# Ones through TensorE while x is loaded, the first norm's sums later in its stream, a third gate row tile on x without norm, and the last norm's two factors in one step

## The chip, the cores and the metric

The kernel runs on one core of a Trainium2 chip. Its engines are TensorE (PE for matmuls, PEld for the loading of their stationary operand), VectorE (DVE), ScalarE (ACT), GpSimd (POOL) and SyncE (SP), which issues nearly all DMAs. The metric is the device time of one execution in microseconds; runs of the same kernel are told by their median.

## The reference, cut to what matters

One layer of a decoder is run for a prompt of 512 tokens and 8 samples of one token each, 520 columns in all, with 1024 features:

- `xn = rmsnorm(h)`, then `z = xn @ w_in`, 66 row tiles of 128 features and one small tile of 8 gate rows. From z come dilated sliding-window attention (with a cache of keys and values for the samples), an mLSTM of 4 heads behind a causal convolution, the gates `og` of its output, and two more gates.
- `h += (sig(g_a) * P_a(attention) + sig(g_b) * P_b(mLSTM)) @ w_out`
- `h += (silu(xf @ w_gate) * (xf @ w_up)) @ w_down` with `xf = rmsnorm(h)`
- `h += sigmoid(rmsnorm(h) @ w_ple_gate) * (p @ w_ple_proj)`
- `y = rmsnorm(h)`, where rmsnorm is `h / sqrt(mean(h^2) + eps) * g`.

All is kept in f32. A row's factor `1/sqrt(mean + eps)` is the same for all features of a token, so `(x*g) @ w` may be computed first and multiplied by it afterwards.

## The kernel before, in words

Activations lie transposed: features on the 128 partitions, 520 tokens along the free axis, in two halves of 260. Each f32 operand of a dense product is split into a rounded part and a rest (`whi`, `wlo` for weights; `x`, `xnh`, `xnl` and so on for activations), and a product is three matmuls: hi by hi, hi by rest, rest by hi. So a row tile of `w_in` (128 by 1024 weights) is 8 slices by 3 products by 2 halves, 48 matmuls of 260 columns, named `pp<-...` after their PSUM pair. The splits are ACT's (`CAST`) and DVE's (`TENSOR_TENSOR wlo`).

No order is written out by hand. A planner (`Clock`, `on`, `Procs`, `dense_to`, lines 52 to 400) holds its own estimate of each engine's time while the program is built. A list of dense products is walked in order; between matmuls every waiting process (attention, mLSTM, norms, evictions) whose condition holds by that estimate issues its next instructions. All helpers record through line 225, so rows of the profile are told apart by tile names. The order is fixed at build time: on the chip each engine takes its instructions strictly in that order.

At the start x comes in 8 tiles (`xr`). For each, ACT writes `x = xr*g` rounded and DVE the rest (`prep`); ACT also squares each (`sq`) and DVE adds the squares (`first_norm`). `norm` sends the sum of squares through two f32 matmuls with a 128 by 128 tile of ones (`b<-sq,onesr`), which adds over the partitions; ACT takes the root and DVE the reciprocal (`rb`). `renorm` then makes the normalised tiles `xn` (`xnh`, `xnl`). So that TensorE has work before `rb` exists, the gate rows `wg` (36 rows wide) and the first row tiles of `og` (`w_in` rows 42, 43, 44) run on x without norm (`pp<-x,...`), and their evictions multiply by `rb` (`ev_tanh` with False, DVE `th<-pp,rb`, then ACT's tanh). Row tiles on `xn` are evicted by ACT's tanh alone.

After that the list has attention rows, the convolution and value rows of head 0 (`j_head(0)`), more attention rows, head 1, the gate tile `j_mo(1, 1)`, head 2 and so on. The attention of the samples runs in between as a process. Its last part takes the values (`kvb`) of the samples from the cache in four batches: three loads of 256 KB by SP, then four groups of three f32 matmuls of 2 columns each (`b<-pT,kvb`; each is two matmuls in the trace). The tiles come from a ring of 5, so the third load of a batch goes to a tile that the batch ahead still reads.

At the end (`ev_pg`, `last_norm`) each of 8 feature tiles per half gets its last addend. Tiles 0 to 5 are squared by ACT and added up by DVE, and ACT multiplies them by the final gain (`gained`). Tiles 6 and 7 are squared and multiplied by the gain on DVE. The sums go through TensorE, then root, reciprocal, and 8 multiplications by it (`h<-h,rb`), each followed by its store.

Of the kernel before, what the change touches and what calls it, by code (L numbers as in the profile page):

```python
# [10 lines left out]
AF = mybir.ActivationFunctionType  # L11
ALU = mybir.AluOpType
# [217 lines left out]
def _body(nc, a, const, sb, psp, drp):  # L230
    ck = Clock()
    V, S_, G_, PE, SP = (Engine(ck, n, e) for n, e in (
        ("dve", nc.vector), ("act", nc.scalar), ("pool", nc.gpsimd), ("pe", nc.tensor), ("sp", nc.sync)))
# [5 lines left out]
    used = dict.fromkeys(("pp", "G", "WK", "b1", "z", "y", "zc", "yc", "S", "P1", "P2", "cm", "hm", "hf", "sw"), 0)  # L239

    def tl(tag, name, shape=None, dt=F32):
        w = WIDTH.get(tag, 520)
        if tag in used:
            used[tag] += 1
        return ck.new(sb.tile(list(shape or (128, w)), dt, name=name, tag=tag, bufs=NB[tag]), tag, NB[tag])
# [8 lines left out]
    def bank(shape=(128, 512)):  # L254
        used["b1"] += 1
        return ck.new(psp.tile(list(shape), F32, name="b1", tag="b1", bufs=4), "b1", 4)
# [7 lines left out]
    def free(n, tag):  # L264
        used[tag] -= n
# [5 lines left out]
    def on(engs, *tiles, lim=None, **rooms):  # L271

        engs = engs.split()

        def ok():
            for tag, n in rooms.items():
                if tag in used and used[tag] + n > NB[tag]:
                    return False
            now = ck.t["pe"]
            for tag, n in rooms.items():  # L280
                i = ck.count.get(tag, 0)
                if any(ck.idle(tag, i + j, NB[tag]) > now + P["SLACK"] for j in range(n)):
                    return False
            if engs[0] == "pe":
                t = now
            else:
                t = min(ck.t[e] for e in engs)
                if t > now + (P["LIM"] if lim is None else lim):
                    return False
                t = max(t, now) + 0.1  # L290
            return all(ck.ready(x) <= t for x in tiles)
        return ok
# [29 lines left out]
    pr = Procs()  # L322
# [46 lines left out]
    def stt(dst, x, sc, y, op0, op1):  # L369
        V.scalar_tensor_tensor(dst, x, sc, y, op0=op0, op1=op1)  # L370

    def tt(dst, x, y, op):
        V.tensor_tensor(dst, x, y, op=op)

    def mul(dst, x, y):
        tt(dst, x, y, ALU.mult)
# [4 lines left out]
    def square(dst, x):  # L381
        S_.activation(dst, x, AF.Square)
# [33 lines left out]
    def job(chunks, rhs, evac, M=128, group=None, half=None, keep=None, two=False):  # L416

        j = dict(chunks=chunks, rhs=rhs, evac=evac, M=M, keep=keep, two=two, halves=(0, 1) if half is None else (half,), nk=sum(c[2] for c in chunks), i=0)
        jobs.append(j)
        if group is None:  # L420
            order.extend((j, c) for c in range(len(chunks)))
        return j
# [327 lines left out]
    def std(name, m):  # L750
        return [(a[name][m, hf], 4 * hf, 4) for hf in range(2)]
# [4 lines left out]
    gmix, gffn, gple, gfin = (par[:, 8 * i:8 * i + 8] for i in range(4))  # L756
# [6 lines left out]
    onesr = const.tile([128, 128], F32R, name="onesr")  # L763
# [8 lines left out]
    def norm(sq, name):  # L772

        yield on("pe", sq, b1=2)
        bk = [bank() for _ in range(2)]
        for h in range(2):
            PE.matmul(bk[h][:, :TH], ones, sq[:, HS[h]], start=True, stop=True)
        for h in range(2):
            S_.activation(rb[:, HS[h]], bk[h][:, :TH], AF.Sqrt, scale=1.0 / 1024, bias=eps_t)
            V.reciprocal(rb[:, HS[h]], rb[:, HS[h]])  # L780
        free(2, "b1")
        free(1, "y")
        flag[name] = True
# [243 lines left out]
    def ev_tanh(tag, key, scaled=True):  # L1027
        room = {tag: 1} if tag in used else {}

        def gen(ps):  # L1030
            if tag in ("P1", "P2"):
                yield lambda: ("loads", 3) in flag
            if scaled:
                yield on("act", ps, lim=P["EVLIM"], **room)
                t = tl(tag, "th", (128, 520))
                S_.activation(p2(t), ps, AF.Tanh, scale=0.5)
                free(1, "pp")
            else:
                yield lambda: "r0" in flag
                yield on("dve", rb, lim=P["EVLIM"], **room)  # L1040
                t = tl(tag, "th", (128, 520))
                V.tensor_tensor(p2(t), ps, p2(rb), op=ALU.mult)
                free(1, "pp")
                yield on("act", t)
                S_.activation(t, t, AF.Tanh, scale=0.5)
            ml[key] = t
        return gen
# [558 lines left out]
    def j_w(m, evac):  # L1606
        job(std("w_in", m), X, evac)
# [8 lines left out]
    def j_mo(h, vt):  # L1616
        j_w(42 + 2 * h + vt, ev_tanh("OB", ("og", h, vt)))

    group([job([(a["wg"][:, 0:4], 0, 4), (a["wg"][:, 4:8], 4, 4)], X0, ev_gates, M=36, group=1),
           job(std("w_in", 42), X0, ev_tanh("OB", ("og", 0, 0), False), group=1)])  # L1620
    for m in (1, 2):
        job(std("w_in", 42 + m), X0, ev_tanh("OB", ("og", m // 2, m % 2), False))

    n_pre = len(order)
# [1 line left out]
    def j_head(h):  # L1626
        for w in range(2):
            for dt in range(2):
                j_w(18 + 8 * w + 2 * h + dt, ev_conv(h, w, dt))
        for vt in range(2):  # L1630
            j_w(34 + 2 * h + vt, ev_vm(h, vt))
# [4 lines left out]
    for p in range(9):  # L1636
        j_attn(1, p)
    j_head(1)
    j_mo(1, 1)
    j_head(2)  # L1640
    j_mo(2, 0)
    j_head(3)
# [20 lines left out]
    SP.dma_start(nst, a["sn"])  # L1663
    V.memset(eps_t, EPS)
    V.memset(ones, 1.0)
    warm = const.tile([128, 1], F32, name="warm")
    S_.activation(warm, eps_t, AF.Sqrt)

# [165 lines left out]
    def add_sq(x, name, w=520):  # L1834
        yield on("act", x, y=1)
        sq = tl("y", "sq")[:, :w]
        square(sq, x)
        yield on("dve", sq)
        n, acc = ssq.get(name, (0, sq))
        if n:  # L1840
            add(acc, acc, sq)
            free(1, "y")
        ssq[name] = n + 1, acc
# [161 lines left out]
    pe = []  # L2005
# [19 lines left out]

    sq_last = [], []

    def gained(m, hm):
        yield on("act", hm, lim=0.0)
        S_.activation(hm, hm, AF.Copy, scale=gfin[:, m:m + 1])  # L2030

    def ev_pg(m, h):
        def gen(ps):
            ps = ps[0]
            yield lambda: "r3" in flag
            yield on("dve", rb, lim=P["EVLIM"], z=1)
            gs = tl("z", "gs3")[:, :TH]
            V.tensor_tensor(gs, ps, rb[:, HS[h]], op=ALU.mult)
            free(1, "b1")
            yield on("act", gs)  # L2040
            S_.activation(gs, gs, AF.Tanh, scale=0.5)
            if m == 7:
                S_.activation(warm, eps_t, AF.Sqrt)
            yield on("dve", gs, ppt[m])
            stt(gs, gs, 1.0, ppt[m][:, HS[h]], ALU.add, ALU.mult)
            hm = hres[m][:, HS[h]]
            yield on("dve", gs)
            stt(hm, gs, 0.5, hm, ALU.mult, ALU.add)
            free(1, "z")
            if m < 6:  # L2050
                yield from add_sq(hm, ("r4", h), TH)
                pr.spawn(gained(m, hm))
            else:
                yield on("dve", hm, y=1)
                sq = tl("y", "sql")[:, :TH]
                V.tensor_tensor(sq, hm, hm, op=ALU.mult)
                sq_last[h].append(sq)
                yield on("dve", hm)
                V.tensor_scalar(hm, hm, gfin[:, m:m + 1], None, op0=ALU.mult)
        return gen  # L2060

    def last_norm(h):
        yield lambda: ssq.get(("r4", h), (0, 0))[0] == 6
        acc = ssq["r4", h][1]
        yield on("pe", acc, b1=1)
        bk = bank()
        PE.matmul(bk[:, :TH], ones, acc, start=True, stop=False)
        free(1, "y")
        for m in range(2):
            yield lambda: len(sq_last[h]) > m  # L2070
            yield on("pe", sq_last[h][m])
            PE.matmul(bk[:, :TH], ones, sq_last[h][m], start=False, stop=m == 1)
            free(1, "y")
        rl = rb2[:, HS[h]]
        S_.activation(rl, bk[:, :TH], AF.Sqrt, scale=1.0 / 1024, bias=eps_t)
        yield on("dve", rl)
        V.reciprocal(rl, rl)
        free(1, "b1")
        for m in range(8):
            yield on("dve", rl, hres[m])  # L2080
            hm = hres[m][:, HS[h]]
            mul(hm, hm, rl)
            store(a["y"][m][:, HS[h]], hres[m][:, HS[h]], None, S_ if h and m % 2 else SP)

    PEI = lambda: pe
# [45 lines left out]
    for h in range(2):  # L2131
        pr.spawn(last_norm(h))
# [146 lines left out]
```

## Time and profile before

| | us |
|---|---|
| median of 3 runs | 1083.18 |
| lowest, highest | 1081.77, 1091.07 |
| the profiled execution's own time | 1080.5 |
| its span in the trace, first to last instruction | 1078.7 |
| PE busy in the span | 1039.9 (96%) |
| DVE busy | 849.8 (79%) |
| ACT busy | 522.7 (48%) |

Busy times of PE contain the time of matmuls at a lower clock, and neighbouring matmuls overlap, so idle time of PE is read from the waits and not from the difference of two sums. A wait in brackets stands at the instruction that waited, with its length and what ended it. `PEclk` is the granted clock as a share of the full one.

### The profile page before, as it was taken

To read this page: it belongs to the slowest core of one execution; us is meant where nothing else is said; L and a number is where in the kernel's file an instruction comes from. 1 tells how busy PE (TensorE), PEld (TensorE's weight loads), DVE (VectorE), ACT (ScalarE), POOL (GpSimd) and SP (SyncE) were. 2 spreads that over 40 slices of the span, in tenths; PEclk is the share of its full clock that TensorE was granted. 3 is DMA by queue.
4 is the path that set the end of the run, shared out by engine and by line. 5 is a ranking of instruction groups with operands and counts; after the bars stand their busy time and mean duration, and the time that the engine had idled before them with its cause. 6 is when DMAs were issued, how large, how long until landed. Compare 5 with 4: busy or idle time off the path is not lost.

```text
span 1078.7 us, 21787 instructions
## 1 busy us (share of the span) xinstructions
PE 1039.9 (96%) x8416; PEld 1018.9 (94%) x8416; DVE 849.8 (79%) x1757; ACT 522.7 (48%) x970; POOL 36.5 (3%) x126
## 2 busy tenths in 40 slices
PE   7999999999998999999999999999999999999996
PEld 6999899999998998999999999999999999999995
DVE  7995569877778689997566678989888888866785
ACT  6545445554555477765333255444344434433663
POOL 0010110001001011000000000000000000000000
PEclk9999999999998899999999999999999999999999
DMA  6356157765946885966757743422332332333331
GB/s 234 119 187 198 59 165 240 276 192 185 278 154 225 275 310 180 328 220 231 255 172 260 246 125 92 151 82 67 120 95 85 118 102 80 113 89 106 98 112 57
DMA packets 91191, 180.21 MB, mean 167 GB/s; under 512 B 11636, under 2 KB 37796, under 8 KB 89680
## 3 DMA queue, kind: packets, MB, share of 16 engines
q1 hardware_dynamic: 90512, 178.29, 51.0%
q8 instruction: 66, 1.08, 0.4%
q10 hardware_dynamic: 576, 0.53, 0.1%
q14 instruction: 37, 0.30, 0.1%
HBM read 163.65 MB, written 59.13 MB: 207 GB/s over the span
## 4 chain that ended last, share of the span: by engine, by line
PE 70%; DVE 13%; DMA 10%; ACT 3%; issue 3%; SPq 1%; POOL 0%; DVEq 0%; ACTq 0%
PE pp L225 40%; PE b L225 30%; DMA ct<-in_sC 3%; DVE wlo L225 2%; DMA raw<-in_w_in 2%; DVE yc L225 1%; DVE ct L225 1%; DMA kb<-mdr 1%; SPq L225 1%; ACT whi L225 1%; DMA out_kvout<-in_cache 1%; DVE junk L225 1%; DMA out_C_p<-cp 1%; DVE sw L225 1%; DMA qb<-mdr 1%
## 5 line engine op out<-in xcount | busy, mean ns | idle before, releaser
L225 ACT CAST whi<-raw 128x512 fp32r<-128x512 f32 (+3 forms) x346 | 205.6, 598 | 284.1 <-PE pp L225 141.6
L225 DVE TENSOR_TENSOR wlo<-raw,whi 128x512 fp32r<-128x512 f32 (+3 forms) x359 | 236.3, 660 | 134.3 <-ACT whi L225 126.5
L225 PE MATMUL b<-piece,whi 128*128 128x260 f32 x1176 | 212.5, 283 | 1.5 <-DVE whi L225 1.4
L225 PE MATMUL pp<-xnh,whi 128*128 128x260 f32 x1008 | 208.5, 288 | 0.0
L225 PE MATMUL pp<-xnh,wlo 128*128 128x260 f32 x1008 | 207.7, 288 | 0.0
L225 PE MATMUL pp<-xnl,whi 128*128 128x260 f32 x1008 | 204.2, 284 | 0.8 <-DVE xnl L225 0.7
L225 PEld LDWEIGHTS b<-piece,whi 128*128 128x128 f32 x1176 | 181.0, 188 | 1.9 <-issue 1.9
L225 PE MATMUL b<-piece,wlo 128*128 128x260 f32 x588 | 166.1, 283 | 0.1
L225 PEld LDWEIGHTS pp<-xnl,whi 128*128 128x128 f32 x1008 | 157.1, 190 | 1.2 <-DVE xnl L225 1.2
L225 PEld LDWEIGHTS pp<-xnh,wlo 128*128 128x128 f32 x1008 | 157.0, 191 | 1.1
L225 PEld LDWEIGHTS pp<-xnh,whi 128*128 128x128 f32 x1008 | 156.7, 190 | 1.2
L225 PEld LDWEIGHTS b<-piece,wlo 128*128 128x128 f32 x588 | 110.7, 188 | 0.4 <-DVE wlo L225 0.4
L225 PE MATMUL pp<-hpl,whi 128*128 128x260 f32 x352 | 70.8, 283 | 0.0
L225 PE MATMUL pp<-hph,whi 128*128 128x260 f32 x352 | 70.6, 282 | 0.0
L225 PE MATMUL pp<-hph,wlo 128*128 128x260 f32 x352 | 70.6, 282 | 0.0
L225 PEld LDWEIGHTS pp<-hph,wlo 128*128 128x128 f32 x352 | 54.3, 188 | 0.0
L225 PEld LDWEIGHTS pp<-hpl,whi 128*128 128x128 f32 x352 | 54.2, 188 | 0.0
L225 PEld LDWEIGHTS pp<-hph,whi 128*128 128x128 f32 x352 | 54.2, 188 | 0.0
L225 ACT CAST whi<-ws 128x512 fp32r<-128x512 f32 x28 | 17.4, 622 | 57.5 <-PE b L225 48.5
L225 DVE SCALAR_TENSOR_TENSOR yc<-zc,par,yc 128x552 f32<-128x552 f32 x48 | 37.7, 786 | 5.1 <-ACT yc L225 4.5
L225 DVE TENSOR_TENSOR uv<-uv,b 128x260 f32<-128x260 f32 (+1 forms) x84 | 40.7, 485 | 0.0
L225 PE MATMUL b<-x3h,wlo 128*128 128x260 f32 x128 | 36.5, 285 | 0.0
(389 smaller groups left out, 1906.3 us busy)
## 6 DMA issues: line engine op xcount, KB each, us to landing
raw<-in_w_in SPq DMA_DIRECT2D x132, 256.0 KB, 2.7
out_kvout<-in_cache SPq DMA_DIRECT2D x64, 512.0 KB, 5.0
raw<-in_w_gate SPq DMA_DIRECT2D x44, 256.0 KB, 4.0
raw<-in_w_up SPq DMA_DIRECT2D x44, 256.0 KB, 3.9
ct<-in_sC SPq DMA_DIRECT2D x32, 256.0 KB, 6.4
out_C_s<-ct SPq DMA_DIRECT2D x32, 256.0 KB, 5.4
raw<-in_w_down SPq DMA_DIRECT2D x32, 256.0 KB, 2.7
out_kvout<-in_cache SPq DMA_DIRECT2D x16, 510.0 KB, 4.8
```

The source lines that it names most:

```text
L225: fn(*args, **kw)
```

## The change

Four edits:

- After the tile of ones is set, 24 matmuls of ones by ones (128 columns) are issued into a PSUM bank that nobody reads.
- `norm` for the first norm waits, in the planner's estimate, until TensorE's time is 1.5 us past the time at which the sum of squares is ready.
- Row tile 45 (`og`, head 1, second half) runs on x without norm with the first three, and is taken out of its place between head 1 and head 2.
- `gained` and its two counterparts on DVE go; the 8 multiplications by the reciprocal become `scalar_tensor_tensor` steps that multiply by the gain (one value per partition, from `par`) and by the reciprocal. The square of tile 6 goes from DVE to ACT.

```diff
@@ norm
         yield on("pe", sq, b1=2)
+        if name == "r0":
+            yield lambda: ck.ready(sq) + 1.5 <= ck.t["pe"] and used["b1"] <= 2
         bk = [bank() for _ in range(2)]
@@ the list of dense products
-    for m in (1, 2):
+    for m in (1, 2, 3):
         job(std("w_in", 42 + m), X0, ev_tanh("OB", ("og", m // 2, m % 2), False))
...
     j_head(1)
-    j_mo(1, 1)
     j_head(2)
@@ start
     V.memset(ones, 1.0)
+
+    wb = bank((128, 128))
+    for _ in range(24):
+        PE.matmul(wb, onesr, onesr, start=True, stop=True)
+    free(1, "b1")
@@ end
-    def gained(m, hm):
-        yield on("act", hm, lim=0.0)
-        S_.activation(hm, hm, AF.Copy, scale=gfin[:, m:m + 1])
...
             if m < 6:
                 yield from add_sq(hm, ("r4", h), TH)
-                pr.spawn(gained(m, hm))
             else:
-                yield on("dve", hm, y=1)
+                yield on("act" if m == 6 else "dve", hm, y=1)
                 sq = tl("y", "sql")[:, :TH]
-                V.tensor_tensor(sq, hm, hm, op=ALU.mult)
+                if m == 6:
+                    square(sq, hm)
+                else:
+                    V.tensor_tensor(sq, hm, hm, op=ALU.mult)
                 sq_last[h].append(sq)
-                yield on("dve", hm)
-                V.tensor_scalar(hm, hm, gfin[:, m:m + 1], None, op0=ALU.mult)
...
-            mul(hm, hm, rl)
+            stt(hm, hm, gfin[:, m:m + 1], rl, ALU.mult, ALU.mult)
```

Since the planner's estimate shifts, the order moves in more places than the edits. Three are shown.

TensorE at the start, before: the norm's two matmuls (`b_294`, `b_295`) stand right behind the gate rows (the 36-wide matmuls), ahead of the second half of the first `og` tile.

```order
L225 MATMUL pp<-x_196,whi 36x260 x2
L225 MATMUL pp<-x_197,whi 36x260 x2
L225 MATMUL pp<-x_196,wlo 36x260 x2
L225 MATMUL b_294<-sq,onesr 128x260
L225 MATMUL b_295<-sq,onesr 128x260
L225 MATMUL pp<-x_174,whi 128x260 x2
L225 MATMUL pp<-x_175,whi 128x260 x2
L225 MATMUL pp<-x_174,wlo 128x260 x2
```

And in the change (`b_330`, `b_331`):

```order
L225 MATMUL pp<-x_221,wlo 36x260 x2
L225 MATMUL pp<-x_199,whi 128x260 x2
L225 MATMUL pp<-x_200,whi 128x260 x2
L225 MATMUL pp<-x_199,wlo 128x260 x2
L225 MATMUL pp<-x_207,whi 128x260 x2
L225 MATMUL pp<-x_208,whi 128x260 x2
L225 MATMUL b_330<-sq,onesr 128x260
L225 MATMUL b_331<-sq,onesr 128x260
L225 MATMUL pp<-x_207,wlo 128x260 x2
```

Ten matmuls of the `og` tile have moved ahead of the norm's two.

TensorE at the fourth and last batch of the samples' values, before: 40 dense matmuls (20 rows, of which the last two stand here) lie between the third batch and the fourth, and the fourth's groups of three have dense matmuls between them.

```order
L225 MATMUL pp<-xnh,whi 128x260 x2
L225 MATMUL pp<-xnl,whi 128x260 x2
L225 MATMUL b_4403<-pT,kvb 128x2 x3
L225 MATMUL pp<-xnh,wlo 128x260 x2
L225 MATMUL b_4403<-pT,kvb 128x2 x3
L225 MATMUL pp<-xnh,whi 128x260 x2
L225 MATMUL pp<-xnl,whi 128x260 x2
L225 MATMUL b_4403<-pT,kvb 128x2 x3
L225 MATMUL pp<-xnh,wlo 128x260 x2
L225 MATMUL b_4403<-pT,kvb 128x2 x3
```

In the change the third batch (`b_4423`) and the fourth (`b_4491`):

```order
L225 MATMUL b_4356<-pT,kvb 128x2 x3
L225 MATMUL pp<-xnh,whi 128x260 x2
L225 MATMUL pp<-xnl,whi 128x260 x2
L225 MATMUL pp<-xnh,wlo 128x260 x2
L225 MATMUL pp<-xnh,whi 128x260 x2
L225 MATMUL pp<-xnl,whi 128x260 x2
L225 MATMUL pp<-xnh,wlo 128x260 x2
L225 MATMUL b_4423<-pT,kvb 128x2 x12
L225 MATMUL pp<-xnh,whi 128x260 x2
L225 MATMUL pp<-xnl,whi 128x260 x2
L225 MATMUL pp<-xnh,wlo 128x260 x2
L225 MATMUL pp<-xnh,whi 128x260 x2
```

Between the second batch (its last group is `b_4356`) and the third there are now 12 dense matmuls, and between the third and the fourth 10 of them and four transposes (`b<-cstA,yc`). From the first batch's first group to the fourth's last there were 124 dense matmuls, and there are 50.

DVE at the end, before: behind the last matmul of the last tile (`gs_14097<-b_14060`), the square and the gain of tile 6 (`h_7928`) and of tile 7 (`h_7930`), then the reciprocal and the multiplications.

```order
L225 TENSOR_TENSOR gs_14097<-b_14060,rb 128x260
L225 TENSOR_TENSOR sq<-sq 128x260
L225 TENSOR_TENSOR sql<-h_7928 128x260
L225 TENSOR_SCALAR h_7928<-h_7928,par 128x260
L225 SCALAR_TENSOR_TENSOR gs_14097<-gs_14097,ppt 128x260
L225 SCALAR_TENSOR_TENSOR h_7930<-gs_14097,h_7930 128x260
L225 TENSOR_TENSOR sql<-h_7930 128x260
L225 TENSOR_SCALAR h_7930<-h_7930,par 128x260
L225 RECIPROCAL rb_13286<-rb_13286 128x260
L225 TENSOR_TENSOR h_7916<-h_7916,rb_13286 128x260
```

And in the change:

```order
L225 TENSOR_TENSOR gs_14110<-b_14074,rb 128x260
L225 TENSOR_TENSOR sq<-sq 128x260
L225 SCALAR_TENSOR_TENSOR gs_14110<-gs_14110,ppt 128x260
L225 SCALAR_TENSOR_TENSOR h_7956<-gs_14110,h_7956 128x260
L225 TENSOR_TENSOR sql<-h_7956 128x260
L225 RECIPROCAL rb_13312<-rb_13312 128x260
L225 SCALAR_TENSOR_TENSOR h_7942<-h_7942,par,rb_13312 128x260
```

Three instructions have left this piece, and each of the 8 multiplications reads a second factor from `par`.

## Rows read from the trace of the kernel before

**Rows 1.** The page's first part: busy time, share, instructions of each engine.

```profile
PE 1039.9 (96%) x8416; PEld 1018.9 (94%) x8416; DVE 849.8 (79%) x1757; ACT 522.7 (48%) x970; POOL 36.5 (3%) x126
```

**Rows 2.** Stretches: busy us (count) of PE, PEld, DVE, ACT, POOL; clock; DMA.

```profile
270.00:485.00 215.00, 204.18 (x1585) 197.97 (x1584) 179.70 (x451) 130.30 (x235) 15.52 (x59) 0.97 0.75 247
485.00:1040.00 555.00, 552.12 (x4582) 549.88 (x4581) 435.71 (x775) 237.73 (x423) 0.00 (x0) 1.00 0.42 135
```

**Rows 3.** Timeline, 0 to 20 us: start, us, engine, out<-in, count, idle before.

```profile
0.84 0.17 DVE L225 MEMSET onesr<- 128x128 f32 x1
5.23 1.44 PE L225 MATMUL pp<-x,whi 128*36 128x260 f32 x4 [5.23 <-ACT x L225]
...
8.83 1.07 PE L225 MATMUL pp<-x,whi 128*36 128x260 f32 x4
...
12.48 0.64 PE L225 MATMUL pp<-x,whi 128*128 128x260 f32 x4
...
14.18 4.71 DVE L225 TENSOR_TENSOR sq<-sq 128x520 f32<-128x520 f32 x6
...
17.27 0.40 PE L225 MATMUL pp<-x,wlo 128*36 128x260 f32 x2
...
18.95 1.14 PE L225 MATMUL b<-sq,onesr 128*128 128x260 f32 x4 [1.28 <-DVE sq L225]
```

**Rows 4.** Timeline, 34 to 41 us, TensorE on the first normalised tiles.

```profile
34.26 0.40 PE L225 MATMUL pp<-xnh,whi 128*128 128x260 f32 x2
...
38.92 0.51 PE L225 MATMUL pp<-xnl,whi 128*128 128x260 f32 x2 [0.65 <-DVE xnl L225]
...
40.74 0.51 PE L225 MATMUL pp<-xnl,whi 128*128 128x260 f32 x2
```

**Rows 5.** Timeline and tile view of the samples' values (kvb), 316 to 338 us.

```profile
316.71 0.72 PE L225 MATMUL b<-pT,kvb 128*128 128x2 f32 x6
...
317.01 0.37 SPq L225 DMA_DIRECT2D kvb<-in_cache  x1
...
320.72 0.72 PE L225 MATMUL b<-pT,kvb 128*128 128x2 f32 x6
...
337.08 0.38 PE L225 MATMUL b<-pT,kvb 128*128 128x2 f32 x2 [0.67 <-DMA kvb<-in_cache]
...
DMA to landing us min/median/max: 4.8/4.9/5.0
```

**Rows 6.** Two stretches of 5 us right behind it.

```profile
340.00:345.00 5.00, 5.00 (x24) 5.00 (x25) 2.29 (x5) 2.66 (x4) 0.66 (x2) 0.50 1.04 401
350.00:355.00 5.00, 3.72 (x18) 3.75 (x19) 4.90 (x16) 1.67 (x3) 0.00 (x0) 0.51 0.61 180
```

**Rows 7.** Waits of TensorE, 345 to 370 us: us in total, times, longest.

```profile
PE b L225 <- DVE nout L225: 1.5, 1, 1.5
PE b L225 <- POOL qkm L225: 1.5, 1, 1.5
```

**Rows 8.** Timeline, 1066 us to the end.

```profile
1067.28 0.42 ACT L225 ACTIVATE gs<-gs 128x260 f32<-128x260 f32 x1 [0.55 <-DVE gs L225]
1067.50 0.42 DVE L225 TENSOR_TENSOR sql<-h 128x260 f32<-128x260 f32 x1
...
1068.23 0.42 DVE L225 SCALAR_TENSOR_TENSOR gs<-gs,ppt 128x260 f32<-128x260 f32 x1
...
1070.89 1.78 DVE L225 RECIPROCAL rb<-rb 128x260 f32<-128x260 f32 x1 [0.92 <-ACT rb L225]
1072.70 2.81 DVE L225 TENSOR_TENSOR h<-h,rb 128x260 f32<-128x260 f32 x8
```

**Rows 9.** Groups by form on DVE: busy us, mean ns, idle before.

```profile
L225 DVE SCALAR_TENSOR_TENSOR xn<-xr,par,rb 128x520 f32<-128x520 f32 x8 | 5.8, 751 | 0.0
...
L225 DVE SCALAR_TENSOR_TENSOR th<-th,pp 128x520 f32<-128x520 f32 x8 | 5.5, 688 | 0.0
L225 DVE TENSOR_TENSOR xnl<-xn,xnh 128x520 fp32r<-128x520 f32 x8 | 5.2, 693 | 0.6 <-ACT xnh L225 0.6
```

## The prediction

> **What bounds the kernel now.** I read first the page's busy times: PE is busy for 1039.9 of 1078.7 us, the next engine, DVE, for 849.8 [rows 1]. A change can win only where TensorE stands still or runs at a lower clock. The stretches say where: from 485 to 1040 us 4582 matmuls fill 555 us, 0.121 us for each, with next to no gap, while from 270 to 485 us PE is busy for 204 of 215 us and the granted clock is 0.97 on the mean [rows 2]. The timeline gives the places that this change touches: the start, the hand-over to the normalised tiles, the attention of the samples around 316 to 338 us, and the tail.
>
> **Start.** The first gate matmul waits until 5.23 us for x. From 8.83 four matmuls take 1.07 us, from 12.48 only 0.64 [rows 3]: a step of 0.217 us against 0.12. The step of 0.217 is that of the lower level (1.2 GHz); it ends between these rows. At 17.27 the last two gate matmuls start, and the norm's sums then wait for DVE until 18.95, for 1.28 us [rows 3].
>
> *24 matmuls of ones.* They can start once the tile of ones is set, at 1.01 us. At 0.121 us each they take 2.9 us, at 0.217 us 5.2 us, so they end between 3.9 and 6.2 us. The late end would push the first gate matmul by 1.0 us. That is covered: between 5.23 and 8.83 us 12 matmuls with 2.6 us of steps take 3.6 us, which leaves 1.0 us idle. A full clock before 8.83 would bring TensorE to the norm's sums sooner, but the sums wait for the sixth addition of squares on DVE (14.18 to 18.89 us) [rows 3], which is fed by x and by ACT and takes nothing from TensorE. So the term is 0 whether or not the clock rises. Without that cover it would be 1.0 us of loss at most, or, if DVE ended earlier, up to 1.0 us of gain.
>
> *Norm's sums later.* Ten matmuls now stand ahead of them: 10 x 0.121 = 1.2 us. Even at the old pace TensorE is through them at 17.51 + 1.21 = 18.72, before 18.95. The sums start when they did, ACT's root and DVE's reciprocal come when they did, and ten matmuls are done: **-1.2 us**. If the sums were ready earlier, their delay would pass to the reciprocal instead.
>
> *Third row tile on x.* Its 48 matmuls are moved, not added. The first normalised matmul, at 34.26 before, comes 48 x 0.121 - 1.2 = 4.6 us later. In front of the last rest `xnl` DVE has one eviction and one weight rest more, 0.69 us each. So the rests come 1.4 us later and their user 4.6 us later, and the wait of 0.65 at 38.92 goes. From 34.26 to 40.74 us 44 matmuls took 6.48 us where 44 x 0.121 = 5.32 would do [rows 4]: **-1.2 us**. The tile's two loads of 256 KB, ACT's two casts and a cache copy move with it; the third row tile's weights are due only 48 matmuls later than the second's, so I cost them at nothing. If they were late, the bound is the 0.65 of the old wait.
>
> **Where the tile is taken out.** This part is dear, and it is no edit: the order shows it. The tile was 5.8 us of work that needs nothing from DVE but its weights, between two heads. Without it the planner puts the samples' four batches into 50 dense matmuls instead of 124. The third load of a batch is issued only once the batch ahead has read its tile: at 317.01, in the last group of the second batch (316.71). A load lands after 4.9 us where its landing was waited for; the group at 320.72, though, waited for nothing, so its third matmul at about 321.2 had its tile after 4.2 us [rows 5]. With 4.9, the third tile is there 5.2 us after the last group's start. In the new order TensorE can fill of this, for batch 2 to 3: the group 0.73, 12 x 0.121 = 1.45, two pairs of the next group 0.48, in all 2.66, wait 2.5 us. Batch 3 to 4: 0.73, 10 x 0.121, four transposes at a dense matmul's step 0.48, and 0.48, in all 2.9, wait 2.3. (Batch 1 to 2 has a dozen mLSTM matmuls between; I take it as covered.) Together 4.8 us against 1.0 before, of which the longer was 0.67 [rows 5]: **+3.8**; with 4.2 us for a landing 3.4, +2.4. I take the middle, +3.1. Against it: while TensorE stands, DVE and POOL go on, and the waits right behind, 1.5 for `nout` and 1.5 for `qkm` [rows 7], can shrink by 0 to 3.0 us; I take half, -1.5. The granted clock was 0.50 from 340 to 345 and 0.51 from 350 to 355 us [rows 6], after TensorE had done the 2-column matmuls with few dense ones between; over the stretch to 485 us 3% of 215, 6.5 us, were lost so [rows 2]. I expect this again, and take 0 for the difference (from -6.5 to +6.5). Sum here **+1.6 us**.
>
> **Tail.** Behind the last tanh (1067.28 + 0.42 = 1067.70) DVE is still at tile 6's square and gain, and goes on at 1068.23 [rows 8]. Both leave: the chain is 0.5 us earlier. Tile 6's square on ACT takes the place of one of ACT's gain steps, ahead of the tanh; hidden. Then 8 steps follow the reciprocal on the path. One that reads a factor per partition takes 751 ns on 128x520, one with a constant 688, a plain product 693 [rows 9]: 0.06 us for the factor, 8 x 0.06 = 0.5 us. Sum **0** (-0.5 if the factor costs nothing on 260 columns). ACT's dozen gain steps in the first half ran beside a TensorE without waits, so they give nothing.
>
> Here a rule speaks against the change. The rows have a `scalar_tensor_tensor` with a constant as fast as a product (688 and 693 ns), both from two f32 sources [rows 9]. The Trainium skill, "Vector Engine (DVE) Microarchitecture Reference", section "Points that are easy to get wrong", says that this instruction with two SBUF sources that are not bf16 runs at half the rate. The trace's `xn<-xr,par,rb` has two such sources and 751 ns, so it does not agree.
>
> **The sum.** The profiled execution took 1080.5 us (span 1078.7), 2.7 below the median of 1083.18. -1.2 - 1.2 + 1.6 + 0 = -0.8: 1079.7 for it, and against the median **1082.4 us**: no change. This kernel's runs differ by some 0.9% (1081.77 to 1091.07), so what is within 1% can't be told from no change.
>
> **Rivals.**
> 1. *Slower: the samples' values hold TensorE, and its clock.* The waits of 4.8 us stand, none behind shrinks, and the emptier stretch keeps the lower level for as long again: -2.4 + 3.8 + 6.5 = +7.9, **1091.1**. For it: only 22 dense matmuls lie between the last three batches. Against: at half clock the matmuls in between fill more of each landing. It decides as soon as waits and lost clock grow by over 2.4 us together. Chance 0.17.
> 2. *Faster: the clock holds.* The two low stretches followed a certain mixture, which is gone; without them -6.5: -2.4 + 1.6 - 6.5 = -7.3, **1075.9**. For it: both were short. Against: the new mixture has fewer columns. Chance 0.10.
> 3. *The start gives nothing.* The planner's 1.5 us is its own estimate; if DVE's additions end early on the chip, the reciprocal is late by what the ten matmuls take, and the old waits come back: +1.6 alone, **1084.8**. Against: 18.95 is set by x. Chance 0.13.
> 4. *The final steps take double.* As a mechanism of this kernel: 8 steps of 0.35 (2.81 for 8 [rows 8]) become 0.70, +2.8 in place of +0.5: -0.8 + 2.3 = +1.5, **1084.7**. Rows 9 speak against it. Chance 0.03. This is what the skill's sentence above would make of it.
>
> The forecast keeps 0.57; its own bounds, from 4.2 us landings with all waits behind gone and the tail's half us (-3.5) to the full waits (+1.4), give 1080 to 1085. The range takes in rival 2 and most of rival 1: **1076 to 1090**. Faster by over 1% (under 1072.3) needs rival 2 with the low bounds, 0.05; slower by over 1% (over 1094) rival 1 with the tail or start lost too, 0.07; within 1%, 0.88.
>
> **What the new profile would show.** Sums still at about 18.95 with a shorter or no wait, ten `x` matmuls ahead; a step of 0.12 before 8.83 us if the ones raise the clock; no wait on `xnl` near 43 us; waits on `kvb` of 3 to 5 us in all, near 320 to 345 us; on ACT no `h<-h,par`; final steps of about 0.41 us on a chain 0.5 us earlier. I am wrong if TensorE waits for `kvb` no longer than before, if the sums start later than 19.5, or if the low clock covers less than 5 or more than 25 us.

## The result: 1% faster, and the profile after

The changed kernel takes 1073.0 us (median of 11 executions, 1070.81 to 1079.78) beside 1083.37 us (median of 11, 1080.26 to 1091.07) on the same chip: a ratio of 0.990, with a 95% interval of 0.9876 to 0.9924. I had forecast 1082.4 us and a range of 1076 to 1090. The gain of 10.4 us is over ten times the 0.8 us of my sum, and most of what the traces place of it lies where my sum had no term.

The profiled executions took 1080.5 us (span 1078.7) and 1072.9 us (span 1071.1). The spans show 7.6 us. The other 2.8 us are that the profiled execution of before lies below its median and the one of after at its own.

The page's first part, after, answers to [rows 1]. The 24 matmuls more are the ones; TensorE's busy time is 1.1 us longer, the span 7.6 us shorter, so it is waiting that went.

```profile
PE 1041.0 (97%) x8440; PEld 1022.7 (95%) x8440; DVE 848.3 (79%) x1749; ACT 518.3 (48%) x963; POOL 40.8 (4%) x126
```

The stretches of after (columns as in [rows 2]): from 485 us on nothing has changed, and the clock from 270 to 485 is no better than before, 0.96 beside 0.97.

```profile
270.00:485.00 215.00, 205.56 (x1604) 200.20 (x1603) 184.08 (x458) 131.57 (x237) 20.41 (x59) 0.96 0.77 249
485.00:1040.00 555.00, 552.45 (x4577) 550.10 (x4577) 435.86 (x778) 237.86 (x420) 0.00 (x0) 1.00 0.41 132
```

**Where the 7.6 us lie.** Since matmuls stand in another order, I compare the start of the same matmul in both timelines and take off 0.121 us for each dense matmul (`pp<-...`) that the change has done more by then (the count is that of the order). What is left is called net below. Four marks do: the first scores of head 0 (`kh,qh`), the end of its attention (`t,cstB`), head 2's `vmh,kwh` and the last `nt`. In the timeline of before:

```profile
91.95 0.33 PE L225 MATMUL b<-kh,qh 64*128 64x128 f32 x1
...
131.40 1.03 PE L225 MATMUL b<-t,cstB 128*128 128x8 f32 x8 [1.45 <-ACT whi L225]
...
367.46 0.28 PE L225 MATMUL b<-vmh,kwh 128*128 128x256 f32 x1
...
478.59 0.62 PE L225 MATMUL b<-nt,onesr 128*128 128x16 f32 x4 [0.55 <-DVE nt L225]
```

And of after:

```profile
97.69 0.33 PE L225 MATMUL b<-kh,qh 64*128 64x128 f32 x1
...
132.67 1.06 PE L225 MATMUL b<-t,cstB 128*128 128x8 f32 x8 [0.25 <-DVE t L225]
...
362.78 0.28 PE L225 MATMUL b<-vmh,kwh 128*128 128x256 f32 x1
...
482.95 0.62 PE L225 MATMUL b<-nt,onesr 128*128 128x16 f32 x4
```

| up to (us, before) | shift | dense matmuls more | net | in this stretch |
|---|---|---|---|---|
| 91.95 | +5.74 | 54 | -0.8 | -0.8 (start) |
| 131.40 | +1.27 | 52 | -5.0 | **-4.2** (head 0's attention) |
| 367.46 | -4.68 | -6 | -4.0 | +1.1 (with the place of the tile taken out) |
| 478.59 | +4.36 | 96 | -7.3 | **-3.3** (heads 2 and 3) |
| 1078.7, end | -7.6 | 0 | -7.6 | -0.3 (with the tail) |

Each column rests on one execution, so I looked at how far executions with one order differ. The kernels with the ones alone and with the end alone (below) have before's order on TensorE up to 1041 us. In their profiled executions head 0's attention takes as long as in that of before within 0.05 us, and the stretch from 367 to 479 us within 0.4 us; but from 131 to 367 us they take 1.8 and 3.4 us longer. So the +1.1 can't be told from nothing, and the 2.8 us that the spans don't show may lie in that stretch; no run shows that they do. A second execution with the change's order (without the ones, below) has -4.2 and -2.7 in the two bold rows.

**Head 0's attention.** Before, 12 transposes of `P` stand in one batch on TensorE:

```
405 L225 MATMUL b_1516<-cstA,P 128x128 x4
406 L225 MATMUL b_1526<-cstA,P 128x128 x4
407 L225 MATMUL b_1536<-cstA,P 128x128 x4
408 L225 MATMUL pp<-xnh,wlo 128x260 x2
```

They take 2.66 us there (116.11 to 118.77), 0.22 each, where four of them at 106.39 took 0.36, 0.09 each. The timelines of TensorE and ACT show why: ACT makes one exponential of `P` in 0.49 us, and each pair of transposes waits for the next one.

```profile
106.39 0.60 PE L225 MATMUL b<-cstA,P 128*128 128x128 f32 x4
106.75 0.49 PE L225 MATMUL pp<-xnh,wlo 128*128 128x260 f32 x2
...
116.11 2.90 PE L225 MATMUL b<-cstA,P 128*128 128x128 f32 x12
118.77 0.48 PE L225 MATMUL pp<-xnh,wlo 128*128 128x260 f32 x2
```

```profile
115.97 0.49 ACT L225 ACTIVATE P<-P,st 128x256 f32<-128x256 f32 x1
...
116.46 0.49 ACT L225 ACTIVATE P<-P,st 128x256 f32<-128x256 f32 x1
...
116.95 0.49 ACT L225 ACTIVATE P<-P,st 128x256 f32<-128x256 f32 x1
```

The list of the matmuls' waits doesn't show them: the modelled end of a matmul, 0.33 us behind its start, covers all but 0.05 us of each gap, while the weight load of the next pair shows 0.3 us. Waits of before from 92 to 138 us (total, times, longest), of the matmuls and of the weight loads:

```profile
PE b L225 <- ACT whi L225: 1.5, 1, 1.5
PE b L225 <- DVE st L225: 0.8, 1, 0.8
PE b L225 <- DVE E L225: 0.4, 1, 0.4
...
PEld b L225 <- ACT P L225: 1.5, 5, 0.3
```

After, no more than two such groups of four stand in a row, and between the others lie other products. All that is left of the waits in the same stretch:

```profile
PE b L225 <- DVE t L225: 0.3, 1, 0.3
PE b L225 <- DVE E L225: 0.2, 1, 0.2
```

That is 2.7 + 1.5 us of waits before and 0.5 after: 3.7 of the 4.2 us. The 1.5 us put down to `whi` stand at the matmul `t,cstB`, which reads `t`. DVE had finished `t` only 0.1 us ahead of that matmul, so DVE's steps up to `t` alone would have held it nearly as long:

```profile
131.11 0.19 DVE L225 TENSOR_TENSOR t<-ex,cstB 128x32 f32<-128x32 f32 x1
```

### The profile page after: what moved, and what is told of

It reads as the page before. It is cut to its first block, busy times and chain, and to the rows that moved or that the text cites. A ratio compares the mean times of both kernels' runs of the same rounds, so it can differ in the third digit from the quotient of the medians.

```text
span 1071.1 us, 21842 instructions
## 1 busy us (share of the span) xinstructions
PE 1041.0 (97%) x8440; PEld 1022.7 (95%) x8440; DVE 848.3 (79%) x1749; ACT 518.3 (48%) x963; POOL 40.8 (4%) x126
## 4 chain that ended last, share of the span: by engine, by line
PE 77%; DVE 12%; DMA 5%; ACT 3%; issue 2%; SPq 0%; POOL 0%; DVEq 0%; ACTq 0%
PE pp L225 45%; PE b L225 32%; DMA raw<-in_w_in 2%; DVE wlo L225 2%; DMA ct<-in_sC 2%; DVE yc L225 2%; DVE ct L225 1%; DVE sw L225 1%; DVE Wf L225 1%; ACT whi L225 1%; DVE z L225 1%; DVE junk L225 1%; SPq L225 0%; DMA kvb<-in_cache 0%; DMA xr<-in_xT 0%
## 5 line engine op out<-in xcount | busy, mean ns | idle before, releaser
L225 PE MATMUL pp<-xnh,whi 128*128 128x260 f32 x992 | 204.2, 287 | 0.0
L225 PE MATMUL pp<-xnh,wlo 128*128 128x260 f32 x992 | 203.5, 287 | 0.0
L225 PE MATMUL pp<-xnl,whi 128*128 128x260 f32 x992 | 199.7, 283 | 0.0
L225 PEld LDWEIGHTS pp<-xnh,wlo 128*128 128x128 f32 x992 | 153.7, 190 | 1.0
L225 PEld LDWEIGHTS pp<-xnh,whi 128*128 128x128 f32 x992 | 153.0, 189 | 1.3
L225 PEld LDWEIGHTS pp<-xnl,whi 128*128 128x128 f32 x992 | 153.5, 189 | 0.0
```

Source lines behind the costliest of these rows:

```text
L225: fn(*args, **kw)
```

## The experiments

Theory A: the order in which the planner puts the attention between the dense matmuls sets the time, and the edits act mostly by shifting the planner's own clock. Theory B: the edits act on the chip (the clock raised by the ones, the fuller start). One thing has to be added to the words on the planner: its estimate sets more than the order. For copies, casts and some multiplications `pick` takes ACT or DVE, whichever the planner thinks is done first. Of the 359 casts `whi<-raw`, DVE has 13 in the trace of before, 15 in that of the change, and 13 to 23 in those below. So "the order" means the order and this choice. Ratios are to the kernel before, with 95% intervals, from up to 12 executions each.

**Each edit alone.** Four kernels, each with one of the four edits of the diff shown above and nothing else.

> The 24 matmuls of ones alone; the order of all other matmuls stays as before. Theory A (the gain of 7.6 us in the profiled spans comes from what the moved tile does to the order of work in head 0's attention, 92 to 131 us, and in the stretch from 287 to 480 us): TensorE reaches the step of 0.12 before 10 us instead of 11.4 to 12, but the norm's sums still wait for DVE's additions and start at 18.9 to 19.4; the time is that of before within 1 us (ratio 0.999 to 1.001). Theory B (the ones raise the clock early and this is carried through to the end): at least 2 us less (ratio 0.998 or lower).

Measured: 0.9997 (0.9982 to 1.0013). TensorE's order is that of before up to 1041 us; the step of 0.12 is there from 11.0 us (before from 12.2), not before 10, and the sums start at 19.22, behind a wait for DVE of 1.9 us (before 1.3). What the ones are worth on the chip can't be told from zero.

> Only the norm's sums are put later, behind ten matmuls of the second row tile on x; the order up to head 0's attention is otherwise as before, but from about 290 us on the planner places a few matmuls otherwise. Theory A: the ten matmuls wait for their own weights, which ACT casts and DVE rests only behind the squares and additions, so the sums start 1 to 2 us later than 18.95 and nothing is won: 0 to +1.5 us (ratio 0.999 to 1.002). My prediction's step: sums at 18.95, 1.2 us less. Theory C (any shift of the planner's clock rolls the order of the attention anew): a difference of 2 us or more of either sign, in the stretch behind 290 us.

Measured: 0.9973 (0.9947 to 0.9999). The sums start at 20.38, 1.4 us later than before, as theory A says, and by 91.95 us the kernel is 0.7 us behind; yet the time is 0.1 to 5.7 us less. What brings that, if it is more than the spread of executions, must lie behind 290 us: at 287 us the kernel is level with before. The one profile (1085.3 us, above this kernel's median of 1083.8) doesn't show it: open.

> Only the row tile is moved (done on x, at the start, and taken out between head 1 and head 2). The order in head 0's attention changes, though not into that of the whole change. Theory A: this alone brings most of the gain, 5 to 8 us less (ratio 0.992 to 0.9955): no waits on xnl near 40 us, and in head 0's attention the transposes of P no longer wait one by one for ACT (2.66 us for 12 before). Theory B: less than 2 us. My prediction's steps for it: -1.2 at the start and +1.6 behind, +0.4.

Measured: 0.9964 (0.9941 to 0.9988), between the theories' numbers. By 131.40 us the tile alone has won 5.0 us net, as much as the whole change. By 256 us (head 1's first `st,E`) it has lost them all again: in head 1's attention TensorE waits 1.7 us for `t`, 0.9 for `pt`, 0.7 for `E`, 0.6 for `P`.

> Only the end is changed (the last norm's two factors in one step, tile 6's square on ACT); the order up to the last matmuls is as before. The chain of the tail is 0.5 us shorter up to the reciprocal. If a factor per partition costs 0.06 us a step, the 8 final steps take 0.5 us more and the sum is 0; if it costs nothing on 260 columns, -0.4 to -0.5; if the step runs at half rate, 8 steps of 0.7 us, +2.3. All theories: within 1 us of before but for the last (ratio 1.002).

Measured: 0.9999 (0.9978 to 1.0021). Nothing that can be told from zero.

The four alone sum to -0.67%; together they give -1.0%. The intervals of the four are too wide to tell these two numbers apart. The next four take parts out.

**The change without the ones** (the loop over `PE.matmul(wb, onesr, onesr, ...)` and its bank are left out).

> The whole change without the 24 matmuls of ones. TensorE's order in head 0's attention is that of the change, behind 290 us a little different. Theory A (the gain is in the order of the attention, not at the start): still 8 to 11 us less than before (ratio 0.990 to 0.9925), with no more than 1 us of waits in 80 to 135 us. Theory B (the ones, by the clock, carry a part that only shows together with the other edits): 5 us less than before or fewer (ratio 0.995 or higher).

Measured: **1.0105** (1.0086 to 1.0125), 1095.8 us. Both theories missed. Up to 290 us it is ahead of the change (net -7.0 at 286.79, where the change has -4.2), then it loses 22 us. In the program it differs from the change by the ones and by the order: on DVE from 252 us, on TensorE from 273 us. Either could be the cause; the pair further down tells them apart.

**The change with the sums where they were** (the two lines in `norm` are left out).

> The whole change with the norm's sums where they were. TensorE's order in head 0's and head 1's attention is now that of the kernel with the moved tile alone, which lost in head 1's attention what it won in head 0's. Theory A (orders decide): 4 to 5 us less than before (ratio 0.995 to 0.9965), with 4 us or more of waits in 190 to 270 us. Theory D (the later sums are a gain by their own work at the start): the first normalised matmul comes 1.2 us later than in the change and nothing else differs, 9 us less than before (ratio 0.9915).

Measured: 0.9959 (0.9931 to 0.9987). As theory A says: TensorE's order in head 0 and head 1 is that of the kernel with the tile alone, and so are the loss in head 1 and the time.

**The taking-out alone.**

```diff
-    j_mo(1, 1)
     j_head(2)
+    j_mo(1, 1)
     j_mo(2, 0)
```

> The kernel before with the row tile taken out between head 1 and head 2, as in the change, but done behind head 2 and not at the start: the order up to 315 us is as before. It measures the taking-out alone, for which my prediction had +1.6 us (waits on kvb 3 to 5 us in all). Theory A' (taking it out costs nothing or gains, since the attention of the samples and head 2 then hide otherwise): 0 to -3 us (ratio 0.997 to 1.000). My prediction's step: ratio 1.0015 with waits on kvb of 3 us or more.

Measured: 1.0006 (0.9986 to 1.0026). The interval holds 0 and my +1.6 us; but the waits on `kvb` are 0.6 us, not 3 to 5. In their place stands a wait of 4.0 us on `nout`. TensorE's waits of this kernel from 270 to 485 us:

```profile
PE b L225 <- DVE nout L225: 6.2, 4, 4.0
...
PE b L225 <- DMA kvb<-in_cache: 0.6, 1, 0.6
```

**The tile ahead of head 0, but on the normalised x.**

```diff
+    j_mo(1, 1)
     for p in range(9):
         j_attn(0, p)
...
     j_head(1)
-    j_mo(1, 1)
```

> The kernel before with the row tile as the first on the normalised x, in place of the third on x without the norm: its 48 matmuls stand ahead of head 0 as in the change, but not at the start. The order in head 0's attention changes once more. Theory A (any order with the waits in head 0's attention spread wins): the waits in 80 to 135 us (2.9 before, and 1.5 more of weight loads that wait for ACT's exponentials) fall by 2 us or more and the time by 2 to 5 us. Theory E (it is the three tiles without the norm, with DVE free of the normalised rests, that win): the wait on xnl at 38.9 us stays and the time is that of before within 1 us (ratio 0.999 to 1.001).

Measured: **1.0142** (1.0111 to 1.0173). Neither theory's number. The wait on `xnl` stays, as said. But "any order wins" is false: here the batch stays (the weight loads wait 1.5 us for `P`), and head 1's attention loses more.

**The order apart from the instructions.** The planner's estimate can be moved without adding or removing work on the chip. In the first kernel it is told of the ones, but they aren't issued; in the second they are issued and it isn't told:

```diff
-        PE.matmul(wb, onesr, onesr, start=True, stop=True)
+        ck.emit("pe", "matmul", (wb, onesr, onesr), {})
```

```diff
-        PE.matmul(wb, onesr, onesr, start=True, stop=True)
+        nc.tensor.matmul(wb, onesr, onesr, start=True, stop=True)
```

> The whole change, with the planner told of the 24 matmuls of ones but none of them issued: TensorE's order is that of the change, row for row, without the ones. It differs from the change without ones (10.5 us slower than before) in the order behind 290 us alone. Theory A (the order that the planner ends with sets the time, not the ones on the chip): like the change, 8 to 12 us less than before (ratio 0.989 to 0.9925). Theory B (the ones on the chip matter): 5 us or more above the change, towards the 1095 us of the change without ones.

> The counterpart: the 24 matmuls of ones are issued, but the planner isn't told of them, so that the order is that of the change without ones. Theory A: 1094 to 1097 us, ratio 1.009 to 1.012, with the same waits behind 310 us (z 5 us, th 4 us) and the same low clock. Theory B: like the change, 1073.

Measured: 0.9900 (0.9866 to 0.9935), 1074.2 us, and 1.0117 (1.0079 to 1.0155), 1097.4 us. Theory A, on both sides. The order of the change without the ones is as fast as the change; the ones without their order are as slow as the change without ones. So of the kernels without ones the one takes 1074.2 and the other 1095.8 us with the same work, ten copies, casts and multiplications of which stand on the other one of ACT and DVE. By the ratios (0.9900 and 1.0105) that is **some 22 us from the order behind 250 us alone**. How much of it the choice of engine brings, no run tells apart. Two stretches of each (columns as in [rows 2]), first the slow one, then the fast one:

```profile
290.00:370.00 80.00, 73.20 (x489) 70.77 (x488) 56.22 (x129) 33.67 (x59) 7.87 (x26) 0.79 0.62 189
...
485.00:620.00 135.00, 125.38 (x975) 123.34 (x974) 87.77 (x176) 54.21 (x95) 0.00 (x0) 0.94 0.65 220
```

```profile
290.00:370.00 80.00, 73.77 (x555) 71.67 (x554) 61.08 (x144) 36.39 (x64) 7.72 (x26) 0.89 0.67 218
...
485.00:620.00 135.00, 133.35 (x1096) 132.67 (x1095) 87.80 (x163) 53.49 (x97) 0.00 (x0) 0.99 0.68 232
```

TensorE is busy as long from 290 to 370 us in both, but at a granted clock of 0.79 against 0.89: 66 matmuls fewer. The slow one's waits from 290 to 620 us name what it stood for:

```profile
PE b L225 <- ACT z L225: 6.3, 3, 5.3
PE pp L225 <- ACT th L225: 4.5, 1, 4.5
PE b L225 <- DVE piece L225: 2.6, 2, 1.8
```

The same means gives two more orders. The kernel **before**, with the planner told of 36 ones that aren't issued:

> The kernel before with the planner told of 36 matmuls of ones that aren't issued, and nothing else: the same instructions as before in another order, which in head 0's attention is that of the kernel with the moved tile alone. Theory A: the waits in head 0's attention fall as they did there, 3 to 4 us won by 131 us; what the new order does further on isn't known (that kernel lost it again in head 1's attention), and the time differs from before by up to 5 us either way, with no change in the work. Theory F (it is the tile done on x ahead of head 0 that takes the waits away, not the order): the stretch up to 131 us takes as long as before within 1 us.

Measured: **1.0090** (1.0059 to 1.0121). No work is added or removed on the chip (14 copies, casts and multiplications go from ACT to DVE and 10 from DVE to ACT), and the time is 10.9 us longer. At the start it loses 3.0 us net: the first gate matmul, at 5.23 us before, comes at 9.40. In this order ACT has the cast of the first `w_in` weights ahead of the first x, and it waits 3.5 us for their load; before, ACT writes the first x at 4.45. ACT in this kernel:

```profile
8.10 0.62 ACT L225 CAST whi<-raw 128x512 fp32r<-128x512 f32 x1 [3.52 <-DMA raw<-in_w_in]
8.62 2.58 ACT L225 ACTIVATE x<-xr,par 128x520 fp32r<-128x520 f32 x4
```

In head 0 the order wins 3.4 us, as said. In head 1 a batch of the same kind forms, with waits of 0.7 us for `pt` and 1.2 for `P`, and then the clock falls: from 235 to 270 us it is 0.71, where before has 1.00. Its profiled rows:

```profile
235.00:270.00 35.00, 31.23 (x172) 28.42 (x172) 19.92 (x54) 12.25 (x35) 2.09 (x6) 0.71 0.46 141
```

The **change**, told of 36 in place of 24 and without the ones on the chip, which puts the batch of 12 back into head 0:

> The change with the planner told of 36 matmuls of ones in place of 24 (none issued): from head 1 on the order is that of the change, but in head 0's attention the 12 transposes of P stand in one batch again, as in the kernel before. Theory A (the batch is what TensorE waited in): 2.5 us for the 12 transposes again and waits of 2 us or more in 80 to 135 us, 3 to 5 us more than the change (ratio to before 0.993 to 0.995). Rival (the gain up to 131 us is the moved work and not the batch): like the change, 0.9900 +- 0.0015.

Measured: 0.9981 (0.9957 to 1.0006): 7.7 us of the gain are gone, more than the 3 to 5 of the theory. The weight loads wait 1.5 us for `P` again, in 5 pieces, and the matmuls 0.8 for `st`, 0.9 for `zc`, 0.4 for `E`. That is the batch's own part, 3.7 us by the table below. The rest has a place too. Against the change with no ones issued, the profiled execution loses 2.0 us net ahead of head 0 (ACT has the cast of the first weights ahead of the first x here too, and the first gate matmul comes at 10.12 us, in that one at 5.35) and 2.2 from 131 to 226 us. These and the batch make 7.8 us. Behind 226 us every engine has the order of the change; the 6.6 us that this execution still loses there (5.7 of them from 287 to 367 us, at a granted clock of 0.82 against 0.89) come from something else, and they are about what it lies above this kernel's median (1088.9 against 1081.9).

**Head 0 in all kernels.** The stretch from the first `kh,qh` to the first `t,cstB`, by TensorE's order in it, with 0.121 us for each dense matmul above or below 126:

| TensorE's order in head 0 | kernels | us | dense | at 126 |
|---|---|---|---|---|
| that of before | before, ones, sums later, end, tile later | 39.45 to 39.49 | 126 | 39.5 |
| change, batch put back | 1 | 37.19 | 112 | 38.9 |
| tile first on the normalised x | 1 | 37.55 | 100 | 40.7 |
| that of the tile alone | tile moved, no sums later, before in another order | 40.13 to 40.14 | 160 | 36.0 |
| that of the change | the change and three without ones or with the planner not told | 34.97 to 34.98 | 124 | 35.2 |

Within a row of several kernels ACT, DVE and POOL have one order in this stretch too. Kernels with different edits and one order agree within 0.04 us; kernels with nearly the same edits and another order differ by 3 to 5. For this stretch that settles it. For 367 to 479 us, where the change wins 3.3 us, no kernel changes that part alone, and it stays argued: the waits there on `nt`, `qkm`, `W3l`, `sqhh` and `sqhl` (3.2 us before from 370 to 485) are nearly gone (0.3), one on `nout` is 0.9 us longer, and one of 0.4 on `W2l` is new.

## Why the prediction was wrong, step by step

- **The step that failed is one that I didn't take.** The sum had terms for the start, for the place where the tile is taken out, and for the tail. Head 0's attention had none: I took the tile as 5.8 us that come earlier and push the rest along, although the order shows the batch of `P` dissolved. The waits there stood in the profile of before, 1.5 put down to `whi`, 0.8 on `st`, and 1.5 more among the weight loads. It is worth -4.2 us here. The new order in heads 2 and 3, -3.3 us, had no term either.
- *Matmuls of ones, 0.* Right on the chip, for the reason given: DVE's additions cover them. They ran from 1.07 to 6.25 us, at the late end of my bounds, and the second tile of x came 0.5 us later in this execution. The step falls from 0.217 to some 0.13 at 9.35 us, and before only at 12.24. I called the step of 0.217 the lower level, and the rows don't bear that out: the granted clock reads 1.00 from 0 to 16 us in both traces, whatever the step. Wrong as a part of the change: in the planner they decide some 22 us.
- *Norm's sums later, -1.2.* Wrong; I had named 19.5 us as the limit, and they start at 20.72. I counted the ten matmuls' columns and not their weights. ACT casts these behind the squares and DVE makes the rests behind the additions, and so both wait in front of the sums. TensorE at the start, after:

```profile
1.07 5.38 PE L225 MATMUL b<-onesr 128*128 128x128 f32 x24 [1.07 <-DVE onesr L225]
...
18.06 0.74 PE L225 MATMUL pp<-x,whi 128*128 128x260 f32 x4 [0.80 <-ACT whi L225]
19.90 0.51 PE L225 MATMUL pp<-x,wlo 128*128 128x260 f32 x2 [1.10 <-DVE wlo L225]
...
20.72 1.04 PE L225 MATMUL b<-sq,onesr 128*128 128x260 f32 x4
```

- *Third row tile on x, -1.2.* Right: no wait on `xnl` is left (from 40.47 to 46 us the pairs of matmuls follow one another every 0.24 us). With the sums' delay the first normalised matmul comes at 40.47, 6.2 us later in place of 4.6; so the start gives -0.8 and not -2.4. This is between rival 3 and the forecast.
- *The tile taken out, +1.6.* The size is near (+1.1 from 131 to 367 us), which is luck: executions with one order differ by more there, and the mechanism is not what I said. `kvb` costs 0.7 us, less than the 1.0 before, which I had named as a sign of being wrong. From the first batch to the last there are 46 dense matmuls, and before 122 (I had counted 50 and 124). The planner put the fourth batch 10 dense matmuls behind the third, the last load is under way while TensorE waits 3.8 us for `nout`, and the fourth batch then waits for no load. TensorE, after:

```profile
333.23 2.39 PE L225 MATMUL b<-pT,kvb 128*128 128x2 f32 x20 [0.74 <-DMA kvb<-in_cache]
...
340.76 1.09 PE L225 MATMUL b<-cstA,yc 128*128 128x128 f32 x4 [3.83 <-DVE nout L225]
```

- *The clock there, no difference.* Right, and rival 2's mechanism is not what happened, though its number was the nearest. The lower level (0.50, 1.2 GHz) is still granted, right behind the wait of 3.8 us:

```profile
340.00:345.00 5.00, 4.24 (x21) 4.28 (x21) 4.89 (x10) 1.96 (x3) 0.00 (x0) 0.50 0.65 209
345.00:350.00 5.00, 5.00 (x25) 4.68 (x25) 4.85 (x15) 1.72 (x3) 0.00 (x0) 0.50 0.46 161
```

- *Tail, 0.* Measured -0.4, from the last `gs` product to the end. Both terms have the size that I gave them. The reciprocal comes 3.58 us behind the last `gs` product (1059.65) in place of 4.07. The 8 steps take 3.29 us in place of 2.81 [rows 8]. So the 0.4 is that the last store is done 2.8 us behind the last step, before 3.2.

```profile
1063.23 1.78 DVE L225 RECIPROCAL rb<-rb 128x260 f32<-128x260 f32 x1 [1.31 <-ACT rb L225]
1065.05 3.29 DVE L225 SCALAR_TENSOR_TENSOR h<-h,par,rb 128x260 f32<-128x260 f32 x8
```

- *Rival 4, the final steps double.* Out: one takes 485 ns on the mean, the plain product before 420, so the second factor costs 0.065 us where I had 0.06. My rows for that were less clean than I said: the 693 ns are a subtraction, and of the 688 ns one source, `pp`, lies in PSUM. The sentence of the Trainium skill named in the prediction ("Vector Engine (DVE) Microarchitecture Reference", section "Points that are easy to get wrong") would make it about 840 (an estimate, twice the product's 420), and this trace doesn't agree. The groups by form on DVE, before and after:

```profile
L225 DVE TENSOR_TENSOR h<-h,rb 128x260 f32<-128x260 f32 x16 | 5.7, 420 | 0.0
```

```profile
L225 DVE SCALAR_TENSOR_TENSOR h<-h,par,rb 128x260 f32<-128x260 f32 x16 | 6.7, 485 | 0.0
```

The bounds failed for the same reason as the sum. I let them take in landings, waits and the clock of the places that I had looked at, and gave 0.05 to a gain above 1%. An order that is made anew from a shifted estimate carries a spread of its own, here from 1073 to 1098 us over ten orders of nearly the same work. That the measured gain of 0.96% still lies within the 1% to which I gave 0.88 is luck: no mechanism that I named brings it.

## What to carry to other kernels

Where a planner or scheduler makes the order from its own clock, an edit is two things: its cost on the chip, and another draw of the order. Compare the whole order of the engine that bounds, batch by batch, see which instructions changed their engine, and price every place where it waited before; then give the draw its own range, which you can measure with kernels that shift only the planner's estimate. And read the waits of the weight loads beside those of the matmuls: a batch that runs at the pace of another engine looks busy.

## What the runs showed of the hardware that I had not expected

- Executions of one program differ by the clock that they are granted. Over 35 executions of the kernel before, the mean granted clock goes from 0.977 to 0.995 and the time from 1094.6 to 1080.3 us; a straight line through them gives 8 us for 0.01. One place where it falls is behind the wait of 1.45 us at 131 us: in the profiled execution of before the clock from 135 to 140 us is 1.00, in that of the kernel with the end alone, with the same order and the same wait, 0.78, and 35 matmuls are done there in place of 45. Of three other kernels with that order and wait, the one with the ones alone has 0.78 there too, and those with the sums later and with the tile later have 1.00. The window of before, then that of the kernel with the end alone:

```profile
135.00:140.00 5.00, 5.00 (x45) 5.00 (x43) 4.79 (x10) 2.83 (x5) 1.11 (x3) 1.00 0.46 159
```

```profile
135.00:140.00 5.00, 5.00 (x35) 5.00 (x35) 3.35 (x6) 1.77 (x3) 0.11 (x1) 0.78 0.02 5
```

- ACT doesn't pass over an instruction that waits for a load. With the planner told of 36 ones ACT stood 3.5 and 4.2 us for the first `w_in` weights (the two kernels above), and only then wrote the first x, with three more behind it without a wait. For that first x TensorE's first gate matmul waited until 9.4 and 10.1 us, against 5.2 before. The eight loads of x were issued in the same order and by 7.2 us in all three.
